# Norms in three slots, and weight tiles split by casting and accumulating transfers

## The chip, the core and the metric

The kernel runs on one core of a Trainium2 chip. The time is the device time of one execution in microseconds (us), the median of several. Its engines are TensorE (PE; its weight loads are PEld), VectorE (DVE), ScalarE (ACT), GpSimd (POOL) and SyncE (SP), each with its own queue that is worked off in order; a queue's instruction waits on semaphores of the other engines and of DMA transfers.

## The reference

One step of a decoder of two layers, for 512 new prompt tokens and 8 x 4 sample tokens (544 in all), model width 1024, in float32. Layer 0 mixes tokens by gated linear attention (GLA), layer 1 by a complex diagonal state-space layer (S5); behind each stands a squared-ReLU MLP of width 4096. Every sublayer stands between two RMS norms:

```
def _rmsnorm(x, g):
    y = xf * lax.rsqrt(jnp.mean(xf * xf, axis=-1, keepdims=True) + EPS)
    return (y * g.astype(jnp.float32)).astype(x.dtype)
...
        h = _rmsnorm(x, prm['g_pre_mix'][i])
        m = mixer(h)                       # GLA or S5
        x = x + _rmsnorm(m, prm['g_post_mix'][i])
        h = _rmsnorm(x, prm['g_pre_mlp'][i])
        f = jnp.square(jax.nn.relu(h @ prm['w_up'][i])) @ prm['w_down'][i]
        x = x + _rmsnorm(f, prm['g_post_mlp'][i])
```

## The kernel before

Features lie on the partitions, tokens along the rows: `X` is 128 x 8 x 544, eight k-slices of 128 features. The tokens are cut in half 0 (288 columns) and half 1 (256).

**Weights and jobs.** The weights are 184 tiles of 128 x 8 x 128 (512 KB). A float32 product is made of three passes in the type float32r: weight high x input high, weight high x input low, weight low x input high (`advance`, L204 to L207, 8 k-slices x 3 = 24 matmuls). A **job** is one tile for one half; `PLAN` lists the blocks of tiles and their order, 368 jobs, counted here from 0. Blocks of 8 tiles (B) run all eight tiles for half 0 and then for half 1; blocks of 4 (Q) do the same with four; the S5 input block runs five tiles for half 0, the same five for half 1, then the last three by turns.

**Splitting a tile** into `wh` (high) and `wl` (low). SP loads the raw tile into one of three buffers (`load_raw`, L97). ACT writes `wh`, the tile rounded to float32r, in two halves of 128x512 (`split_w`, L119); POOL, and in some stages DVE, subtract: `wl = raw - wh` (L126, L124). While a norm is under way (`dve_win`), POOL does all of the subtraction. `plan` (L131) decides by a table ahead of which job each half tile is split: as soon as its slot in a ring of 5 (or among 4 extra ones) is free, at most 9 jobs ahead. When the second half is split, the raw tile three further on is loaded.

**The queue order** is written by hand: `job` puts the planned splits first, then the 24 matmuls, and `finish` then the evacuation of the job's PSUM bank, the functions deferred to that job (`self.after`), and what is late. So on each engine the norm's instructions stand between the evacuations of successive jobs, and nothing overtakes.

**The norm between two sublayers** (`post`, L322). When the last tile of a block's half is done, `m_done` has summed the squares of the block's output `acc` into `S1`; a matmul by ones sums them over partitions (L258), `rsqrt` (L261) makes the factor `rp` (ACT two passes, DVE three). Then come steps of one to two k-slices each, one step a job, five steps for half 0 and at most six for half 1. A step (L336) does on DVE `xm = acc * g * rp` (L340) and `X += xm` (L343), then the step before's `xl` (`pre_lo`, L311), and on ACT `xh = X * g` (L301) and the square of `X` (L279) into the PSUM bank that `xm` had; the sum of that square into `S2` (DVE, L280) is put off to the next job. `xh` and `xl` are the inputs of the next block; the factor of the second norm (`rs`) is applied at that block's evacuations.

Such norms stand at three places where the next block needs `xh` and `xl` at once: **norm 1** between the GLA's output block (tiles 24 to 31, jobs 48 to 63) and the first MLP (tiles from 32, jobs from 64), **norm 2** between that MLP and the S5 input (tiles 96 to 103, jobs 192 to 207), and **norm 3** between the gated output of S5 (tiles 112 to 119, jobs 224 to 239) and the second MLP (tiles from 120, jobs from 240). In each, half 0's norm runs beside the jobs of half 1 of the block before, and half 1's norm beside the jobs of half 0 of the next.

Of the kernel before, what the change touches and what calls it, by code (L numbers as in the profile page):

```python
# [9 lines left out]
F32 = mybir.dt.float32  # L10
# [8 lines left out]
KD = D // 128  # L19
# [7 lines left out]
C_ID, C_ONE, C_TRI, C_END = 0, 128, 256, 384  # L27
V_PRE, V_POST, V_MPRE, V_MPOST, V_HEAD, V_GATE, V_EPS, V_END = 0, 16, 32, 48, 64, 72, 76, 77
RING, RAW, LEAD = 5, 3, 9

# [4 lines left out]
Q, B = (4, QUAD), (8, BIG)  # L37
MLP = [B, Q, Q] + [Q, Q, Q, Q] * 2 + [Q, Q, B]
PLAN = [Q] * 6 + [B] + MLP + [(8, S5IN)] + [Q, Q, B] + MLP
EXTRA_FROM = (6, 6 + len(MLP), 8 + len(MLP))  # L40


def f32(ap):
    return ap.bitcast(F32)
# [33 lines left out]
class Builder:  # L78
# [16 lines left out]


    def load_raw(self, t):  # L97
        if t < self.n_tiles:
            r = self.p_raw.tile([128, KD, 128], F32, tag="raw", name="raw")
            self.nc.sync.dma_start(r, self.io["w"][t].rearrange("p (k m) -> p k m", k=KD))  # L100
            self.raw[t] = r

    def split_w(self, t, part=None, cast_only=False):

        if part is None:
            self.split_w(t, 0)
            self.split_w(t, 1)
            return
        nc = self.nc
        r = self.raw[t]  # L110
        if part == 0 and (t, 0) not in self.is_cast:
            pool = self.p_x if self.in_x[t] else self.p_w
            self.wh[t] = pool.tile([128, KD, 128], F32R, tag="wh", name="wh")
            self.wl[t] = pool.tile([128, KD, 128], F32R, tag="wl", name="wl")
        h, l = self.wh[t], self.wl[t]
        d = self.dve_ks if self.dve_win is None else self.dve_win
        a, b, c = part * 4, part * 4 + d, part * 4 + 4
        if (t, part) not in self.is_cast:
            nc.scalar.activation(h[:, a:c], r[:, a:c], AF.Copy)  # L119
        if cast_only:  # L120
            self.is_cast.add((t, part))
            return
        if b > a:
            nc.vector.tensor_sub(l[:, a:b], r[:, a:b], f32(h[:, a:b]))  # L124
        if c > b:
            nc.gpsimd.tensor_sub(l[:, b:c], r[:, b:c], f32(h[:, b:c]))  # L126
        if part:
            del self.raw[t]
            self.load_raw(t + RAW)

    def plan(self):  # L131

        first, last, self.in_x = {}, {}, {}
        j = t = 0
        opened = 0
        ready = {}
        for b, (n, order) in enumerate(PLAN):
            if b in EXTRA_FROM:
                opened = j
            for i, _ in order:  # L140
                first.setdefault(t + i, j)
                last[t + i] = j
                j += 1
            for i in range(n):
                self.in_x[t + i] = order is BIG and i >= 4
                ready[t + i] = opened if self.in_x[t + i] else 0
            t += n
        assert t == self.n_tiles
        slots = {False: [0] * RING, True: [0] * 4}
        self.split_at = defaultdict(list)  # L150
        at = 0
        for t in range(self.n_tiles):
            free = slots[self.in_x[t]]
            soon = free.pop(0) + 1
            if t > 3:
                soon = max(soon, ready[t], first[t] - LEAD)
                at = max(soon, min(at + 2, first[t] - 5))
                assert at < first[t], t
                self.split_at[at].append((t, 0))
                self.split_at[min(at + 1, first[t] - 1)].append((t, 1))  # L160
            free.append(last[t])
        self.wjob = 0
        self.block = 0
        self.flat = [(b, h) for b, (_, order) in enumerate(PLAN) for _, h in order]
# [157 lines left out]
    def post(self, hf, g_post, g_pre, sink=None):  # L322

        nc = self.nc
        c0, c1 = HALF[hf]
        n = c1 - c0
        R = {}

        def start():
            r = self.p_t.tile([128, 288], F32, tag="rp", name="rp", bufs=1)  # L330
            self.rsqrt(self.col_sums(self.S1[hf][:, :n], n), n, 1.0 / D, r[:, :n])
            R["r"] = r

        fresh = []

        def step(ks):  # L336
            ms = [self.bank("xm")[:, :n] for k in ks]
            for k, m in zip(ks, ms):
                gk = self.vec[:, g_post + k:g_post + k + 1]
                nc.vector.scalar_tensor_tensor(m, self.acc[:, k, c0:c1], gk, R["r"][:, :n], op0=OP.mult, op1=OP.mult)  # L340
            for k, m in zip(ks, ms):
                x = self.X[:, k, c0:c1]
                nc.vector.tensor_add(x, x, m)  # L343
            if g_pre is not None:
                for k in fresh:
                    self.pre_lo(hf, k, g_pre)
                fresh[:] = ks
                for k, m in zip(ks, ms):
                    self.pre_hi(hf, k, g_pre, False, True, None, m)
            if sink:  # L350
                for k in ks:
                    sink(hf, k)

        at = self.wjob - 1
        blk = self.flat[at][0]
        nxt = [j for j in range(at, len(self.flat)) if self.flat[j][0] > blk and self.flat[j][1] == hf]
        gap = nxt[0] - at if nxt else 4
        lead = 1
        if hf:
            self.defer(lead, start)  # L360
        else:
            self.mid[self.jobs + 1].append(start)
        self.defer(0, lambda: setattr(self, "dve_win", DK[hf]))
        if hf:
            self.defer(8, lambda: setattr(self, "dve_win", None))
        slots = min(gap - 1 - lead, SL[hf])
        for i in range(slots):
            part = list(range(KD))[i * KD // slots:(i + 1) * KD // slots]
            self.defer(lead + i, lambda part=part: step(part))
        self.defer(lead + slots, lambda: step([]))  # L370
        if g_pre is not None:
            late = HL[hf]
            self.hold.update(range(self.jobs + gap, self.jobs + gap + late))
            self.before_evac[self.jobs + gap + late].append(lambda: self.pre_scale(hf))
# [42 lines left out]
    def m_done(self, m, hf, g_post, g_next, sink=None):  # L417

        c0, c1 = HALF[hf]
        n = c1 - c0  # L420
        if sink and hf:
            self.last_done(m, g_post, sink)
            return
        self.square_into(self.S1[hf][:, :n], self.acc[:, m, c0:c1], n, m == 0,
                         self.nc.vector, hf and m < KD - LT)
        if m == KD - 1:

            self.nc.scalar.activation(self.spare, self.vec[:, V_EPS:V_EPS + 1], AF.Abs_reciprocal_sqrt)
            self.post(hf, g_post, g_next, sink)
# [1132 lines left out]
```

## Time and profile before

| | us |
|---|---|
| median of 3 runs (lowest, highest) | 1340.35 (1338.58, 1344.46) |
| profiled execution | 1346.7 |
| its span, first to last instruction | 1344.9 |
| PE busy | 1293.1 |
| DVE busy | 763.9 |
| ACT busy | 621.2 |
| POOL busy | 467.4 |

The profiled execution's own time is 1.8 us over its span, and 6.35 us over the median. Its mean granted clock of TensorE is 0.984. In the rows quoted below a name like `xl<-X,vec,xh` is output and inputs; "x2" is a count; what stands in brackets is how long the engine stood idle before and who released it.

### The profile page before, as it was taken

To read this page: it belongs to the slowest core of one execution; us is meant where nothing else is said; L and a number is where in the kernel's file an instruction comes from. 1 tells how busy PE (TensorE), PEld (TensorE's weight loads), DVE (VectorE), ACT (ScalarE), POOL (GpSimd) and SP (SyncE) were. 2 spreads that over 40 slices of the span, in tenths; PEclk is the share of its full clock that TensorE was granted. 3 is DMA by queue.
4 is the path that set the end of the run, shared out by engine and by line. 5 is a ranking of instruction groups with operands and counts; after the bars stand their busy time and mean duration, and the time that the engine had idled before them with its cause. 6 is when DMAs were issued, how large, how long until landed. Compare 5 with 4: busy or idle time off the path is not lost. (4 is left out here: it accounts for less than half of the span.)

```text
span 1344.9 us, 25669 instructions
## 1 busy us (share of the span) xinstructions
PE 1293.1 (96%) x9966; PEld 1265.0 (94%) x9966; DVE 763.9 (57%) x1749; ACT 621.2 (46%) x1412; POOL 467.4 (35%) x603
## 2 busy tenths in 40 slices
PE   7999999999999999999998988998999999999996
PEld 6899999999999999999998987997999999999996
DVE  6866564678436667666567787346821332332446
ACT  6634354565426646555444343445533432432432
POOL 4443254543371111121422443443324333343241
PEclk9999899999999999999999999999999999999998
DMA  6242222322325555545315686331222223232222
GB/s 192 95 130 86 97 93 83 115 81 73 110 77 163 157 162 173 167 144 160 104 59 193 196 263 205 98 110 63 64 79 90 86 79 108 79 91 83 79 63 67
DMA packets 80681, 155.29 MB, mean 115 GB/s; under 512 B 9040, under 2 KB 45264, under 8 KB 79536
## 3 DMA queue, kind: packets, MB, share of 16 engines
q1 hardware_dynamic: 80560, 153.66, 36.9%
q8 instruction: 78, 1.28, 0.4%
q14 instruction: 43, 0.35, 0.1%
HBM read 128.17 MB, written 25.46 MB: 114 GB/s over the span
## 5 line engine op out<-in xcount | busy, mean ns | idle before, releaser
L126 POOL TENSOR_TENSOR wl<-raw,wh 128x384 fp32r<-128x384 f32 (+3 forms) x351 | 346.9, 1000 | 637.7 <-ACT wh L119 631.1
L206 PE MATMUL held<-xl,wh 128*128 128x256 f32 (+1 forms) x1344 | 393.2, 293 | 11.1 <-DVE xl L311 11.1
L206 PE MATMUL held<-xh,wh 128*128 128x256 f32 (+1 forms) x1344 | 395.2, 294 | 0.1
L206 PE MATMUL held<-xh,wl 128*128 128x256 f32 (+1 forms) x1344 | 389.9, 290 | 0.0
L206 PE MATMUL held<-hh,wh 128*128 128x256 f32 (+1 forms) x1024 | 296.2, 289 | 1.1 <-ACT acc L396 1.1
L206 PE MATMUL held<-hl,wh 128*128 128x256 f32 (+1 forms) x1024 | 296.1, 289 | 0.0
L206 PE MATMUL held<-hh,wl 128*128 128x256 f32 (+1 forms) x1024 | 294.7, 288 | 0.0
L119 ACT ACTIVATE wh<-raw 128x512 fp32r<-128x512 f32 x368 | 219.9, 621 | 125.0 <-PE held L206 75.7
L206 PEld LDWEIGHTS held<-xl,wh 128*128 128x128 f32 x1344 | 256.6, 191 | 13.9 <-DVE xl L311 13.4
L206 PEld LDWEIGHTS held<-xh,wh 128*128 128x128 f32 x1344 | 256.8, 191 | 2.8 <-issue 1.2
L206 PEld LDWEIGHTS held<-xh,wl 128*128 128x128 f32 x1344 | 256.1, 191 | 0.0
L124 DVE TENSOR_TENSOR wl<-raw,wh 128x128 fp32r<-128x128 f32 (+3 forms) x324 | 170.9, 539 | 111.5 <-ACT wh L119 104.2
L206 PEld LDWEIGHTS held<-hh,wh 128*128 128x128 f32 x1024 | 193.2, 189 | 3.0 <-ACT acc L396 1.3
L206 PEld LDWEIGHTS held<-hl,wh 128*128 128x128 f32 x1024 | 193.0, 188 | 0.1
L206 PEld LDWEIGHTS held<-hh,wl 128*128 128x128 f32 x1024 | 192.7, 188 | 0.0
L388 ACT ACTIVATE r<-r 128x256 f32<-128x256 f32 (+1 forms) x128 | 55.0, 430 | 162.2 <-DVE r L386 162.1
L398 DVE TENSOR_TENSOR acc<-held,acc 128x288 f32<-128x288 f32 (+1 forms) x96 | 42.1, 439 | 119.9 <-PE held L206 119.9
L390 DVE TENSOR_TENSOR hl<-r,hh 128x256 fp32r<-128x256 f32 (+1 forms) x128 | 60.7, 474 | 84.6 <-ACT hh L389 84.3
L386 DVE SCALAR_TENSOR_TENSOR r<-held,rs 128x256 f32<-128x256 f32 (+1 forms) x128 | 55.9, 437 | 70.7 <-PE held L206 70.2
L206 PE MATMUL held<-zl,wh 128*128 128x288 f32 (+1 forms) x240 | 69.0, 288 | 1.2 <-DVE zl L1298 1.1
L206 PE MATMUL held<-zh,wh 128*128 128x288 f32 (+1 forms) x240 | 69.5, 289 | 0.0
L206 PE MATMUL held<-zh,wl 128*128 128x288 f32 (+1 forms) x240 | 68.8, 286 | 0.0
(387 smaller groups left out, 2010.7 us busy)
## 6 DMA issues: line engine op xcount, KB each, us to landing
raw<-in_w SPq DMA_DIRECT2D x184, 512.0 KB, 3.6
S<-in_h SPq DMA_DIRECT2D x4, 1024.0 KB, 4.9
out_gla_s<-S SPq DMA_DIRECT2D x4, 1024.0 KB, 3.8
wd<-blk SPq DMA_DIRECT2D x16, 256.0 KB, 2.6
wd<-cs SPq DMA_DIRECT2D x16, 256.0 KB, 3.3
qd<-blk SPq DMA_DIRECT2D x16, 256.0 KB, 2.6
qt<-qd SPq DMA_DIRECT2D x16, 256.0 KB, 3.9
wt<-wd SPq DMA_DIRECT2D x12, 256.0 KB, 4.3
```

Of the source, the lines that this page charges most:

```text
L119: nc.scalar.activation(h[:, a:c], r[:, a:c], AF.Copy)
L124: nc.vector.tensor_sub(l[:, a:b], r[:, a:b], f32(h[:, a:b]))
L126: nc.gpsimd.tensor_sub(l[:, b:c], r[:, b:c], f32(h[:, b:c]))
L206: self.nc.tensor.matmul(ps, a[:, k], cols(b, k), start=(k == 0 and i == 0), stop=(k == KD - 1 and i == 2))
L386: nc.vector.scalar_tensor_tensor(r[:, :n], ps, 0.0, self.rs[hf][:, :n], op0=OP.max, op1=OP.mult)
L388: nc.scalar.activation(r[:, :n], r[:, :n], AF.Square)
L390: self.late.append(lambda: nc.vector.tensor_sub(hl[:, m, c0:c1], r[:, :n], f32(h)))
L398: nc.vector.tensor_add(a, ps, a)
```

## The change

It has two parts.

*Norms in three slots.* A step is cut in three: `residual` (DVE: `xm`, `X`), `high` one job later (ACT: `xh`, squares), `low` one job after that (DVE: `xl`, sums of squares). The squares go to tiles in SBUF, the first one straight into `S2`. For half 1 the number of steps is at most `gap - 3`, where it was `gap - 2`: six as before where the gap is nine jobs, three instead of four in norm 2. The squares of `acc` in half 1, but the first and the last two, are put off by a job.

*Eighteen tiles by transfers.* The tiles 32 to 39, 96, 97 and 120 to 127 have no raw load and no subtraction. POOL issues a transfer from the weights in DRAM into `wh`, which casts to float32r (`load_high`); three jobs later ACT writes `wl = -wh` in one pass of 128x1024, and POOL issues a second transfer of the same tile that adds it to `wl` (`add_low`). `plan` asks for six jobs between the first transfer and the first use.

```diff
+LANDS = 3
+BY_DMA = {*range(32, 40), 96, 97, *range(120, 128)}
...
     def load_raw(self, t):
-        if t < self.n_tiles:
+        if t < self.n_tiles and t not in BY_DMA:
...
+        if part in ("high", "low"):
+            if not cast_only:
+                (self.load_high if part == "high" else self.add_low)(t)
+            return
...
-            self.load_raw(t + RAW)
+            self.load_raw(self.raw_after(t))
+
+    def raw_after(self, t):
+        ts = [u for u in range(t + 1, self.n_tiles + RAW) if u not in BY_DMA]
+        return ts[RAW - 1]
+
+    def source(self, t):
+        return self.io["w"][t].rearrange("p (k m) -> p k m", k=KD)
+
+    def load_high(self, t):
+        pool = self.p_x if self.in_x[t] else self.p_w
+        self.wh[t], self.wl[t] = (pool.tile([128, KD, 128], F32R, tag=n, name=n) for n in ("wh", "wl"))
+        self.nc.gpsimd.dma_start(self.wh[t], self.source(t))
+
+    def add_low(self, t):
+        self.nc.scalar.activation(self.wl[t], f32(self.wh[t]), AF.Copy, scale=-1.0)
+        self.nc.gpsimd.dma_start(self.wl[t], self.source(t), accum_op=OP.add)
...
-            if t > 3:
+            if t in BY_DMA:
+                soon = max(soon, ready[t], first[t] - 3 * LANDS)
+                self.split_at[soon].append((t, "high"))
+                self.split_at[soon + LANDS].append((t, "low"))
+                assert soon + 2 * LANDS < first[t], t
+            elif t > 3:
...
-        def step(ks):
+        squares = {}
+
+        def residual(ks):
             ms = [self.bank("xm")[:, :n] for k in ks]
...
-            if g_pre is not None:
-                for k in fresh:
-                    self.pre_lo(hf, k, g_pre)
-                fresh[:] = ks
-                for k, m in zip(ks, ms):
-                    self.pre_hi(hf, k, g_pre, False, True, None, m)
...
+        def high(ks):
+            for k in ks:
+                x = self.X[:, k, c0:c1]
+                nc.scalar.activation(self.xh[:, k, c0:c1], x, AF.Copy, scale=self.vec[:, g_pre + k:g_pre + k + 1])
+            for k in ks:
+                q = self.p_t.tile([128, 288], F32, tag="sq", name="sq", bufs=5)[:, :n] if k else self.S2[hf][:, :n]
+                nc.scalar.activation(q, self.X[:, k, c0:c1], AF.Square)
+                squares[k] = q
+
+        def low(ks):
+            for k in ks:
+                self.pre_lo(hf, k, g_pre)
+            for k in ks:
+                if k:
+                    s = self.S2[hf][:, :n]
+                    nc.vector.tensor_add(s, s, squares.pop(k))
...
-        slots = min(gap - 1 - lead, SL[hf])
+        slots = min(gap - 2 - lead, SL[hf]) if g_pre is not None else min(gap - 1 - lead, SL[hf])
         for i in range(slots):
             part = list(range(KD))[i * KD // slots:(i + 1) * KD // slots]
-            self.defer(lead + i, lambda part=part: step(part))
-        self.defer(lead + slots, lambda: step([]))
+            self.defer(lead + i, lambda part=part: residual(part))
+            if g_pre is not None:
+                self.defer(lead + i + 1, lambda part=part: high(part))
+                self.defer(lead + i + 2, lambda part=part: low(part))
...
-        self.square_into(self.S1[hf][:, :n], self.acc[:, m, c0:c1], n, m == 0,
-                         self.nc.vector, hf and m < KD - LT)
+        square = lambda: self.square_into(self.S1[hf][:, :n], self.acc[:, m, c0:c1], n, m == 0,
+                                          self.nc.vector, hf and m < KD - LT)
+        if hf and 0 < m < KD - 2:
+            self.after[self.jobs + 1].insert(0, square)
+        else:
+            square()
```

ACT's queue in norm 3, half 0, before, from the evacuation of job 233 (`s`, a sigmoid; `acc` is the evacuation of job 234). Lines are those of each program; the number behind a name tells one buffer from the next.

```order
L1383 ACTIVATE s_10925<-held_10900 128x256
L279 ACTIVATE sq_10928<-acc_10158 128x256
L301 ACTIVATE xh_79<-X_78,vec_76 128x288
L279 ACTIVATE xm_10930<-X_78 128x288
L301 ACTIVATE xh_79<-X_78,vec_76 128x288
L279 ACTIVATE xm_10931<-X_78 128x288
L119 ACTIVATE wh_10896<-raw_10662 128x512
L1380 ACTIVATE acc_10158<-held_10945 128x256
```

The same place now:

```order
L1431 ACTIVATE s_10912<-held_10887 128x256
L382 ACTIVATE xh_79<-X_78,vec_76 128x288
L385 ACTIVATE S20_83<-X_78 128x288
L154 ACTIVATE wl_10811<-wh_10810 128x1024
L1428 ACTIVATE acc_10154<-held_10928 128x256
L310 ACTIVATE sq_10954<-acc_10154 128x256
```

Behind job 233 now stands the first k-slice, whose `X` DVE made behind job 232, where the second and third stood, whose `X` is made behind job 233 itself. The half tile of `wh` has become a whole pass `wl<-wh`, and the square of `acc` stands one job later.

DVE's queue at the same place before, from the product that ends the evacuation of job 233 (`acc<-acc,s`) to the step behind job 234:

```order
L1384 TENSOR_TENSOR acc_10158<-acc_10158,s_10925 128x256
L340 SCALAR_TENSOR_TENSOR xm_10930<-acc_10158,vec_76,rp_10877 128x288
L340 SCALAR_TENSOR_TENSOR xm_10931<-acc_10158,vec_76,rp_10877 128x288
L343 TENSOR_TENSOR X_78<-X_78,xm_10930 128x288
L343 TENSOR_TENSOR X_78<-X_78,xm_10931 128x288
L311 SCALAR_TENSOR_TENSOR xl_80<-X_78,vec_76,xh_79 128x288
L280 TENSOR_TENSOR S20_83<-S20_83,xm_10931 128x288
L280 TENSOR_TENSOR S20_83<-S20_83,xm_10930 128x288
L280 TENSOR_TENSOR S11_82<-S11_82,sq_10928 128x256
L340 SCALAR_TENSOR_TENSOR xm_10974<-acc_10158,vec_76,rp_10877 128x288
```

And now:

```order
L1432 TENSOR_TENSOR acc_10154<-acc_10154,s_10912 128x256
L371 SCALAR_TENSOR_TENSOR xm_10917<-acc_10154,vec_76,rp_10867 128x288
L371 SCALAR_TENSOR_TENSOR xm_10918<-acc_10154,vec_76,rp_10867 128x288
L374 TENSOR_TENSOR X_78<-X_78,xm_10917 128x288
L374 TENSOR_TENSOR X_78<-X_78,xm_10918 128x288
L342 SCALAR_TENSOR_TENSOR xl_80<-X_78,vec_76,xh_79 128x288
L371 SCALAR_TENSOR_TENSOR xm_10963<-acc_10154,vec_76,rp_10867 128x288
L374 TENSOR_TENSOR X_78<-X_78,xm_10963 128x288
L1432 TENSOR_TENSOR acc_10154<-acc_10154,s_10994 128x256
L311 TENSOR_TENSOR S11_82<-S11_82,sq_10954 128x256
L342 SCALAR_TENSOR_TENSOR xl_80<-X_78,vec_76,xh_79 128x288 x2
```

The sums into `S20` have moved behind the `xl` of their slices, and no longer stand between one step's `X` and the next one's `xm`.

POOL's queue through norm 3 and after, before (the first two rows are the end of S5's scan, the third holds the tiles up to the norm, the fourth those beside it, the fifth the rest of the program's):

```order
L1362 TENSOR_TENSOR area<-area 128x256
L1363 TENSOR_TENSOR S_82<-S_82,area 128x256
L126 TENSOR_TENSOR wl<-raw,wh 128x384 x25
L126 TENSOR_TENSOR wl<-raw,wh 128x512 x16
L126 TENSOR_TENSOR wl<-raw,wh 128x384 x111
```

And now:

```order
L133 TENSOR_TENSOR wl<-raw,wh 128x384 x24
L150 DMA wh<-in_w 128x1024 x2
L155 DMA wl<-in_w 128x1024
L150 DMA wh<-in_w 128x1024 x2
L155 DMA wl<-in_w 128x1024 x2
L150 DMA wh<-in_w 128x1024
L155 DMA wl<-in_w 128x1024
L150 DMA wh<-in_w 128x1024 x2
L155 DMA wl<-in_w 128x1024
L150 DMA wh<-in_w 128x1024
L155 DMA wl<-in_w 128x1024 x3
L133 TENSOR_TENSOR wl<-raw,wh 128x512
```

Sixteen subtractions are gone, one of the third row and fifteen of the fourth; one of 128x512 is left behind the norm, and sixteen transfers stand there instead, each tile's second one queued ahead of later tiles' first ones.

More of the change, by code (lines that the diff above doesn't have):

```diff
@@ L332, in start @@
             R["r"] = r
-        fresh = []
-        def step(ks):
+        squares = {}
+        def residual(ks):
             ms = [self.bank("xm")[:, :n] for k in ks]
```

## The prediction

> **What bounds the kernel now.** I read the page first: PE is busy for 96% of the span, so only the other 4%, and what is slow inside the 96%, can be won. The waits of PE come next; the largest of them is this row (engine and line, whom it waits for: us in total, times, longest).
>
> ```profile
> PE held L206 <- DVE xl L311: 11.1, 10, 3.2
> ```
>
> PE waits for `xl`, the low half of a normed input, so the waits are at the starts of the blocks behind the three norms that feed further blocks. Then I cut PE's stretches there, from the first matmul of a job to the first of a later one, beside two undisturbed stretches (borders, us, PE busy and matmuls, granted clock, DMA share, GB/s).
>
> ```profile
> 294.70:300.10 5.40, 4.46 (x30) 1.00 0.23 46
> 322.70:327.40 4.70, 3.44 (x29) 1.00 0.00 0
> 707.20:713.50 6.30, 4.48 (x30) 1.00 0.35 105
> 726.50:736.90 10.40, 8.25 (x52) 0.84 0.28 107
> 880.96:906.55 25.59, 25.59 (x195) 1.00 0.44 135
> 909.88:926.72 16.84, 16.84 (x146) 1.00 0.21 64
> 929.65:945.50 15.85, 10.81 (x53) 0.78 0.26 78
> 964.69:975.00 10.31, 8.22 (x52) 0.83 0.00 0
> ```
>
> Rows 5 and 6 hold 8 jobs of half 0 and 6 of half 1: 3.20 us and 2.81 us a job at a clock of 1.00. The other rows are jobs 64, 72, 192, 197+198, 240+241 and 248+249. A job behind a norm also carries column sums, which this change leaves. What one costs at full clock shows inside job 232 (start, us, operation):
>
> ```profile
> 909.04 0.65 PE L258 MATMUL sums<-S,cst 128*128 128x288 f32 x2
> 909.31 0.49 PE L206 MATMUL held<-zh,wh 128*128 128x256 f32 x1
> 909.64 0.28 PE L206 MATMUL held<-zl,wh 128*128 128x256 f32 x1
> ```
>
> From 909.04 to 909.64 where one matmul takes 0.12: about 0.5 us. Jobs 64, 192 and 240 carry two sums, jobs 72, 197 and 248 one. So the stretches lose, against their own pace:
>
> - norm 1 (before the first MLP): 5.40 - 4.2 = 1.2, and 4.70 - 3.3 = 1.4; together 2.6 us
> - norm 2 (before S5): 6.30 - 4.2 = 2.1, and 10.40 - 6.1 = 4.3; together 6.4 us
> - norm 3 (before the last MLP): 15.85 - 7.4 = 8.45, and 10.31 - 6.1 = 4.2; together 12.65 us
>
> 21.6 us in all, which is the ceiling of what the change can win. Part of it is a granted clock of 0.78 to 0.84 in the rows in which PE stood still; a wait that goes takes that with it.
>
> **Why the norms are late.** In norm 3 (905 to 975 us) two things stand in the waits.
>
> ```profile
> ACT xh L301 <- DVE X L343: 14.9, 10, 2.4
> PE held L206 <- DVE xl L311: 6.6, 5, 3.2
> ```
>
> First, ACT stands 14.9 us for the `X` that DVE has to make in the same step: a step goes DVE, ACT, and back to DVE. Second, DVE is stretched wherever POOL splits a weight tile (two POOL rows, then four of DVE):
>
> ```profile
> 934.06 1.26 POOL L126 TENSOR_TENSOR wl<-raw,wh 128x512 fp32r<-128x512 f32 x1 [3.37 <-ACT wh L119]
> 936.65 2.82 POOL L126 TENSOR_TENSOR wl<-raw,wh 128x512 fp32r<-128x512 f32 x2 [1.33 <-ACT wh L119]
> ...
> 916.49 0.43 DVE L1384 TENSOR_TENSOR acc<-acc,s 128x256 f32<-128x256 f32 x1 [3.15 <-ACT s L1383]
> 922.42 0.94 DVE L311 SCALAR_TENSOR_TENSOR xl<-X,vec,xh 128x288 fp32r<-128x288 f32 x2
> 934.28 1.32 DVE L1384 TENSOR_TENSOR acc<-acc,s 128x256 f32<-128x256 f32 x1 [1.26 <-ACT s L1383]
> 936.38 1.96 DVE L311 SCALAR_TENSOR_TENSOR xl<-X,vec,xh 128x288 fp32r<-128x288 f32 x2
> ```
>
> The same DVE operation takes 0.43 us alone and 1.32 beside POOL's subtraction, the pair of `xl` 0.94 and 1.96. DVE ends the `xl` of job 240 at 938.34, where PE, which began that job at 929.65, wanted the last ones (k = 6, 7 of 8, three quarters of 3.2 us in) at about 932.
>
> **The change, norm 3, half 0.** The eight tiles 120 to 127 no longer pass through POOL, so the stretched rows lose 0.9 to 1.0 us each. The steps become three slots: DVE's residual, one job later ACT's `xh` and squares, one job later DVE's `xl` and sums, so neither engine waits inside a slot. What is left is DVE's own work, and it has to fit. `rp`, from which it starts, ends at 912.3; one row of each kind in this window:
>
> ```profile
> 911.84 0.45 DVE L270 SCALAR_TENSOR_TENSOR rp<-na,ny 128x288 f32<-128x288 f32 x1
> ...
> L343 DVE TENSOR_TENSOR X<-X,xm 128x288 f32<-128x288 f32 x8 | 3.3, 446 | 0.1
> L280 DVE TENSOR_TENSOR S<-S,xm 128x288 f32<-128x288 f32 x7 | 3.2, 450 | 1.8 <-ACT xm L279 1.7
> ```
>
> Up to the last `xl` stand 8 `xm` and 8 `X` at about 0.45, 8 `xl` at 0.47, five sums of the new squares at 0.45, and three products and three sums of half 1 at 0.43: 7.2 + 3.8 + 2.3 + 2.6 = 15.9 us, so 928.2 at the earliest. The slots follow PE's jobs: the last `xl` stands behind job 238, which ends at 926.7 (row 6 ends there), and behind ACT's last `xh`. I put it at about 928.5, before the 932 that PE needs. The wait and the low clock behind it go: 8.45 us, of which I take 7.5.
>
> **Half 1** is tight. From `rp` at 948.41 to the last `xl` at 969.80 DVE needs 21.4 us; four rows in between are stretched:
>
> ```profile
> 947.99 0.42 DVE L270 SCALAR_TENSOR_TENSOR rp<-na,ny 128x256 f32<-128x256 f32 x1
> ...
> 950.90 1.52 DVE L311 SCALAR_TENSOR_TENSOR xl<-X,vec,xh 128x256 fp32r<-128x256 f32 x1
> 952.34 1.55 DVE L390 TENSOR_TENSOR hl<-r,hh 128x288 fp32r<-128x288 f32 x1
> ...
> 954.51 2.26 DVE L340 SCALAR_TENSOR_TENSOR xm<-acc,vec,rp 128x256 f32<-128x256 f32 x2
> ...
> 959.45 1.39 DVE L340 SCALAR_TENSOR_TENSOR xm<-acc,vec,rp 128x256 f32<-128x256 f32 x1
> ...
> 968.93 0.87 DVE L311 SCALAR_TENSOR_TENSOR xl<-X,vec,xh 128x256 fp32r<-128x256 f32 x2
> ```
>
> Against about 0.45 a piece that is 1.05 + 1.1 + 1.35 + 0.95 = 4.4 us, which leaves 17.0. `rp` ends 7.1 us after job 241 begins:
>
> ```profile
> 941.34 0.80 PE L206 MATMUL held<-xh,wh 128*128 128x288 f32 x1
> ```
>
> Seven jobs of 3.20 later job 248 begins, and wants its last `xl` 2.1 us into it: 24.5 us, against 7.1 + 17.0 = 24.1. It fits by 0.4 us, so of the 4.2 us I take 3.5. Norm 3: 11.0 us.
>
> **Norm 1** has the same shape with tiles 32 to 39: of 2.6 us I take 2.2.
>
> **Norm 2** has only tiles 96 and 97 by transfer; 98 to 100 are split on POOL as before, a few jobs sooner. Half 1 has three slots instead of four, since the block is followed after six jobs. Its rows on DVE:
>
> ```profile
> 708.13 2.50 DVE L311 SCALAR_TENSOR_TENSOR xl<-X,vec,xh 128x288 fp32r<-128x288 f32 x2
> ...
> 716.56 0.42 DVE L270 SCALAR_TENSOR_TENSOR rp<-na,ny 128x256 f32<-128x256 f32 x1
> ...
> 722.91 0.86 DVE L280 TENSOR_TENSOR S<-S,xm 128x256 f32<-128x256 f32 x2
> ...
> 730.83 0.88 DVE L311 SCALAR_TENSOR_TENSOR xl<-X,vec,xh 128x256 fp32r<-128x256 f32 x2
> ```
>
> The stretched pair of 2.50 (1.56 over the 0.94 above) falls at a time when POOL now has nothing, which brings `rp` forward by about 1.6. From `rp` to the last `xl` (716.98 to 731.71) DVE is full without any help from POOL; all that goes is three sums that now stand behind the last `xl`, 3 x 0.43 = 1.3 us. PE still waits there and still gets the low clock. 1.6 + 1.3 = 2.9 us.
>
> **The sum:** 11.0 + 2.2 + 2.9 = 16.1 us. The profiled execution took 1346.7 us (span 1344.9) and the median shown is 1340.35; I take the same 16 us off both: 1330.6 for a profiled one, **1324.3** for the median.
>
> **What is added.** On ACT one pass of 128x1024 stands where two of 128x512 stood; the row of the latter in norm 3 is
>
> ```profile
> L119 ACT ACTIVATE wh<-raw 128x512 fp32r<-128x512 f32 x17 | 10.2, 615 | 0.0
> ...
> L279 ACT ACTIVATE xm<-X 128x288 f32<-128x288 f32 x7 | 2.8, 395 | 0.0
> ...
> L275 ACT ACTIVATE S<-X 128x288 f32<-128x288 f32 x1 | 0.4, 428 | 0.0
> ```
>
> so it costs the same 1.1 to 1.2 us, now in a piece and with a wait: it needs the first transfer landed, and behind it in ACT's order stand evacuations. The squares keep their passes and go to SBUF instead of PSUM (0.43 against 0.40 us, rows 3 and 2), which is nothing. SP's queue loses 18 loads, and nothing behind them comes later. POOL issues 36 transfers, in order; the second of each tile waits for ACT there, and the next tile's first stands behind it. Neither operation is in the trace. The nearest rows are the raw loads of the same 512 KB and the queue as a whole:
>
> ```profile
> raw<-in_w SPq DMA_DIRECT2D x184, 512.0 KB, 3.6
> ...
> DMA to landing us min/median/max: 3.2/3.6/8.3
> q1 hardware_dynamic: 80560, 153.66, 36.9%
> ```
>
> Landing: no quicker than 3.2 us, and for the accumulating one, which fetches what it adds and what it adds to, at most twice the slowest load, 16.6. I take 3.6 and about 7. The plan leaves three jobs (9 us) between the first transfer and ACT's pass, and four or more from there to the first use (12 us, less some 3.5 in which ACT gets to it): both fit. Throughput: 0.369 x 16 x 1344.9 us for 153.66 MB is 1.7 us of all 16 engines for 512 KB, so a tile's two transfers are 1.7 + 3.4 = 5.1 us if the second counts double; eight tiles take 41 us of the 16 jobs (48 us) from job 231 to job 247. At zero they cost nothing; above 6 us a tile they are late.
>
> The Trainium skill, "Collectives: The Full Stack", section "The bandwidth ceiling", says that the add in a transfer costs nothing itself, but needs two reads on the same ring. No run here shows it; by it the pair is those 5.1 us, with no add on top.
>
> **Rivals.**
>
> *POOL holds DVE up all the same.* If building a transfer on POOL stretches DVE as its subtraction does, norm 3's and norm 1's collisions stay (16 transfers for 16 subtractions, 0.9 us each, a good half of them on the late path). Left are the slots' share and norm 2: about 6 us, 1334. For it: every POOL row of these windows has a stretched DVE row beside it. Against it: the issue touches none of the tiles that DVE reads. The Trainium skill, "SBUF — State Buffer", section "Who interferes with whom", says that a DVE instruction with two SBUF inputs collides with a GpSimd instruction that reads SBUF, not with one that only writes. The rows above agree with the first half; the second no trace here shows, and by it this rival falls.
>
> *ACT becomes late.* ACT's pass waits for a landing of over 9 us, or simply stands as 1.1 us ahead of an evacuation, and the slots behind it slip by a job. That gives back half 1 of norm 3 and more, and leaves 1337 to 1341, no change. It speaks for it that half 1 fits by 0.4 us only.
>
> *The accumulating transfers are slow: slower than before.* They share one queue. At 8 us a tile, eight take 64 us of the 48: 16 us of PE waiting for `wl` in norm 1 and again in norm 3, 32 lost against 16 won, 1356. It decides from 6 us a tile. Against it: the DMA share in these stretches is 0 to 0.44.
>
> **How the numbers follow.** Forecast 0.66; POOL still in the way 0.14; ACT late 0.10; slow transfers 0.10. The forecast's own range is 1319 (19 us won) to 1331. A measurement of this kernel tells 0.5% (6.7 us) from no change: faster is the forecast and half of the first rival, 0.73; the same 0.17; slower 0.10. The range that leaves out two in ten reaches from 1318 to 1339.
>
> **What will show it.** Right: PE's waits for `xl` at the starts of norms 1 and 3 are gone, the clock is 1.00 there, no DVE row of norm 3 exceeds 0.6 us, job 197 still waits. Wrong: rows "PE held <- DMA wl", or ACT waiting for `wh` from DMA (transfers); DVE rows over 1 us beside POOL's DMA rows (first rival); PE waiting for `xl` with undisturbed DVE rows (ACT late).

## The result, and the profile after

| | before | after |
|---|---|---|
| median of 6 runs each (lowest to highest), us | 1342.51 (1338.58 to 1346.79) | 1329.23 (1325.58 to 1331.35) |
| profiled execution, us | 1346.7 | 1328.09 |
| its span, us | 1344.9 | 1326.3 |

The ratio is 0.9904, with a 95% interval from 0.9887 to 0.9921: the change saves about 13 us. The prediction was 1324.3 us, with a range of 1318 to 1339.

The list of waits of the changed kernel (engine and line, whom it waits for: us in total, times, longest) has the last four of these rows; the first two are of the kernel before, where PE also waited 11.1 us for `xl`:

```profile
PE sums L258 <- DVE S L280: 2.2, 3, 1.5
ACT xh L301 <- DVE X L343: 44.8, 27, 3.6
...
PE held L237 <- DVE xl L342: 0.4, 1, 0.4
PE sums L289 <- DVE S L394: 4.5, 4, 1.3
PE sums L289 <- DVE S L311: 1.4, 1, 1.4
ACT xh L382 <- DVE X L374: 11.1, 8, 3.4
```

So PE's wait for `xl` is gone but for 0.4 us, and a smaller one has grown from 2.2 to 5.9 us: for `S`, the sums of squares, which DVE now adds behind the last `xl`, and without which PE cannot do the column sum of the new norm.

The stretches of the prediction in the changed kernel (jobs 64, 72, 192, 197+198, 240+241, 248+249; borders, us, PE busy and matmuls, granted clock, DMA share, GB/s):

```profile
288.75:292.67 3.92, 3.92 (x31) 1.00 1.10 257
315.25:319.81 4.56, 3.39 (x28) 1.00 0.00 0
699.32:706.53 7.21, 4.57 (x30) 1.00 0.37 120
719.51:727.57 8.06, 6.75 (x52) 1.00 0.15 57
921.93:929.25 7.32, 7.32 (x55) 1.00 1.08 306
948.63:956.28 7.65, 6.47 (x52) 1.00 0.21 59
```

The clock is 1.00 in all six. Jobs 64 and 240+241 are without a gap; they were 5.39 and 15.85. Row 3 is longer than before (6.27), and rows 2, 3, 4 and 6 still hold gaps of 1.2 to 2.6 us.

**Where the 13 us are.** I take the difference of the two traces' job starts, piece by piece. From job 64 to 75 it grows by 1.6 us (norm 1), from 191 to 199 by 1.4 (norm 2), from 239 to 251 by 11.2 (norm 3). That makes 14.2 us. Between 199 and 212, in the S5 stage, 1.8 us come back; in the ten traces of the experiments the same piece takes from 106.4 to 110.0 us (before 108.1), in no order that follows what was changed, so I leave it out of the account. The two spans differ by more, 18.6 us: another 5.9 us lie ahead of job 48, in GLA code that the change doesn't touch (last section).

**What is left in the gaps.** Norm 2 of the changed kernel, DVE and POOL (start, us, engine, line, operation; idle time before and who ended it):

```profile
690.82 2.58 DVE L371 SCALAR_TENSOR_TENSOR xm<-acc,vec,rp 128x288 f32<-128x288 f32 x2
...
698.62 2.06 DVE L394 TENSOR_TENSOR S<-S,sq 128x288 f32<-128x288 f32 x2
...
702.13 1.89 DVE L394 TENSOR_TENSOR S<-S,sq 128x288 f32<-128x288 f32 x2
```

```profile
691.47 1.60 POOL L133 TENSOR_TENSOR wl<-raw,wh 128x512 fp32r<-128x512 f32 x1
...
699.08 1.29 POOL L133 TENSOR_TENSOR wl<-raw,wh 128x512 fp32r<-128x512 f32 x1 [1.47 <-ACT wh L126]
702.38 1.32 POOL L133 TENSOR_TENSOR wl<-raw,wh 128x512 fp32r<-128x512 f32 x1 [2.01 <-ACT wh L126]
```

Three DVE pairs, 0.94 to 1.01 us each where nothing collides, are stretched to 1.9 to 2.6 beside the subtractions of tiles 98 to 100. Two of them are sums of squares: these now read two tiles in SBUF. In norm 3 one place is left, at 949.21, where the pair of `xl` and the two sums behind it are stretched beside POOL's subtraction of tile 128, just when job 248 needs them. Norm 1 has the same beside tile 40, at 315.82 (norm 3 first, then norm 1):

```profile
949.21 1.97 DVE L342 SCALAR_TENSOR_TENSOR xl<-X,vec,xh 128x256 fp32r<-128x256 f32 x2
951.10 1.75 DVE L394 TENSOR_TENSOR S<-S,sq 128x256 f32<-128x256 f32 x2
949.21 1.29 POOL L133 TENSOR_TENSOR wl<-raw,wh 128x512 fp32r<-128x512 f32 x1 [9.65 <-ACT wh L126]
...
315.82 1.91 DVE L342 SCALAR_TENSOR_TENSOR xl<-X,vec,xh 128x256 fp32r<-128x256 f32 x2
316.02 2.57 POOL L133 TENSOR_TENSOR wl<-raw,wh 128x512 fp32r<-128x512 f32 x2 [9.65 <-ACT wh L126]
```

### The profile page after: what moved, and what is told of

Same layout as the page of the kernel before. It is cut to its first block, busy times and chain, and to the rows that moved or that the text cites. A ratio compares the mean times of both kernels' runs of the same rounds, so it can differ in the third digit from the quotient of the medians.

```text
span 1326.3 us, 25660 instructions
## 1 busy us (share of the span) xinstructions
PE 1281.2 (97%) x9966; PEld 1256.4 (95%) x9966; DVE 748.7 (56%) x1746; ACT 618.9 (47%) x1394; POOL 445.7 (34%) x603
## 5 line engine op out<-in xcount | busy, mean ns | idle before, releaser
L133 POOL TENSOR_TENSOR wl<-raw,wh 128x384 fp32r<-128x384 f32 (+3 forms) x315 | 300.1, 964 | 552.0 <-ACT wh L126 547.1
L237 PE MATMUL held<-xl,wh 128*128 128x256 f32 (+1 forms) x1344 | 389.2, 290 | 0.4 <-DVE xl L342 0.4
L126 ACT ACTIVATE wh<-raw 128x512 fp32r<-128x512 f32 x332 | 198.4, 622 | 124.4 <-PE held L237 78.7
L237 PEld LDWEIGHTS held<-xh,wh 128*128 128x128 f32 x1344 | 254.0, 189 | 2.4 <-issue 1.4
L237 PEld LDWEIGHTS held<-xl,wh 128*128 128x128 f32 x1344 | 253.6, 189 | 1.0 <-DVE xl L342 0.6
L237 PEld LDWEIGHTS held<-xh,wl 128*128 128x128 f32 x1344 | 253.1, 188 | 0.2 <-DMA wl<-in_w 0.2
L434 DVE TENSOR_TENSOR hl<-r,hh 128x256 fp32r<-128x256 f32 (+1 forms) x128 | 56.4, 440 | 83.8 <-ACT hh L433 83.3
```

The lines of the kernel that those rows point to most:

```text
L237: self.nc.tensor.matmul(ps, a[:, k], cols(b, k), start=(k == 0 and i == 0), stop=(k == KD - 1 and i == 2))
L434: self.late.append(lambda: nc.vector.tensor_sub(hl[:, m, c0:c1], r[:, :n], f32(h)))
```

## The experiments

All times are medians of 4 to 12 runs; the ratio is to runs of the kernel before that were taken beside them. A table of job lengths from the traces (start to start, us) comes first, since most of the reading is done in it. "Both" is the changed kernel. Each kernel has one trace, of one of its executions.

| jobs | before | both | slots alone | transfers alone | transfers, high first | 23 tiles, high first |
|---|---|---|---|---|---|---|
| 64, 65 | 8.78 | 7.31 | 11.48 | 7.31 | 7.31 | 7.31 |
| 68, 69 | 6.40 | 6.40 | 6.40 | 13.41 | 7.53 | 6.40 |
| 72, 73 | 7.71 | 7.61 | 6.66 | 6.13 | 6.13 | 6.13 |
| 192, 193 | 9.65 | 10.60 | 10.76 | 11.58 | 9.64 | 7.31 |
| 197, 198 | 10.42 | 8.06 | 7.81 | 6.83 | 9.91 | 8.92 |
| 240, 241 | 15.85 | 7.32 | 9.96 | 9.46 | 9.45 | 7.32 |
| 243 to 245 | 9.60 | 9.79 | 9.60 | 16.80 | 12.57 | 9.60 |
| 248, 249 | 10.34 | 7.65 | 11.77 | 6.13 | 6.13 | 6.13 |
| median, us | 1342.51 | 1329.23 | 1342.17 | 1342.56 | 1331.65 | 1323.76 |

### Each part by itself

```diff
-BY_DMA = {*range(32, 40), 96, 97, *range(120, 128)}
+BY_DMA = set()
```

> The changed kernel with no tile by transfer (BY_DMA empty): all 184 tiles are loaded by SP and split by ACT and POOL again; the three slots and the squares in SBUF stay. Theory 1, POOL's subtractions are the larger cause: the stretched DVE rows (1.3 to 2.0 us beside POOL) are back in norms 1 and 3, job 240 takes 8 us or more again, PE waits for xl 6 to 10 us in all, and the time is 1335 to 1339 (3 to 7 us won against the kernel before, my prediction put 6). Theory 2, the waits of ACT and DVE for each other in a step are the cause: job 240 stays near 4 us, the time stays at 1329 to 1331. Theory 3, the squares in SBUF make more DVE work collide with POOL (the sums of squares now have two inputs in SBUF), which takes back what the slots win: 1340 or more.

Measured: 1342.17 us, ratio 1.0002 (0.9981 to 1.0023). Nothing is won in the medians; theory 1's 3 to 7 us and theory 2 fall, and the time is the one that theory 3 gave. In the table the slots win at jobs 240 and 197, and give back at jobs 64 and 65, at 192 and at 248. By the one trace they don't give back all of it: over the three pieces used above it is 4.5 us shorter than the trace of the kernel before (1.7 lost in norm 1, 1.5 and 4.6 won in norms 2 and 3). The medians of 12 and 23 runs don't show these 4.5 us, and their interval ends at about 2.5 us won; where the rest goes stays open. DVE's rows of norm 1 (jobs 55 to 74) by form, first of the kernel before, then of the slots alone (count, busy us, mean ns):

```profile
L311 DVE SCALAR_TENSOR_TENSOR xl<-X,vec,xh 128x288 fp32r<-128x288 f32 x8 | 5.4, 707 | 0.0
...
L280 DVE TENSOR_TENSOR S<-S,xm 128x288 f32<-128x288 f32 x7 | 3.2, 454 | 3.1 <-ACT xm L279 3.0
```

```profile
L342 DVE SCALAR_TENSOR_TENSOR xl<-X,vec,xh 128x288 fp32r<-128x288 f32 x8 | 7.8, 1008 | 0.0
L394 DVE TENSOR_TENSOR S<-S,sq 128x288 f32<-128x288 f32 x7 | 6.2, 888 | 0.3
```

The slots put `xl` and the sums where POOL subtracts: 2.4 and 3.0 us more for these two forms, against 2.2 us less for the `xm` of both halves. Of the 42 sums of squares of `X` in the whole trace, two start while POOL subtracts in the kernel before, with the square in PSUM, and none takes over 0.6 us; in the run of the slots nine do, with the square in SBUF, and all nine take 1.3 to 1.6 us. So the slots changed both how many sums meet a subtraction and where the square stands. That fits the rule of the Trainium skill, "SBUF — State Buffer", section "Who interferes with whom": a DVE instruction with at most one SBUF input doesn't contend with GpSimd (two-port modes aside), one with two contends with a GpSimd instruction that reads SBUF. The rows 454 and 888 agree with it on both sides.

The other part (the diff shows its core; the old number of steps and the sums of `acc`'s squares at their old place belong to it):

```diff
-        def residual(ks):
...
+        def step(ks):
...
+            for k, m in zip(ks, ms):
+                self.pre_hi(hf, k, g_pre, False, True, None, m)
```

> The kernel before with the eighteen tiles by transfer and nothing else: steps of DVE, ACT, DVE, squares in PSUM, sums of acc's squares at their old place. Theory 1 (POOL's subtractions are the larger cause): the DVE rows of norm 3 are undisturbed, its last xl of half 0 comes about 7 us earlier (eight POOL rows of 0.9 us each), which is nearly the 6.3 us by which it was late, so job 240 takes 4 to 6 us and the time is 1329 to 1333. Theory 2 (ACT and DVE waiting for each other in a step): ACT still waits some 30 us or more for X, job 240 takes 8 us or more, the time is 1336 to 1340. If the parts add, this run's gain and that of the slots alone make 13 us together; if either is enough, each wins nearly 13; if both are needed, they win less than 13 together.

Measured: 1342.56 us, ratio 1.0000 (0.9981 to 1.0018). Nothing again, so the parts win 13 us together and none apart. But the table says why. The collisions do go: norm 3 (jobs 231 to 249) has 15 transfers issued on POOL and no DVE row stretched beside one,

```profile
L371 DVE SCALAR_TENSOR_TENSOR xm<-acc,vec,rp 128x288 f32<-128x288 f32 x8 | 3.9, 520 | 0.0
L342 DVE SCALAR_TENSOR_TENSOR xl<-X,vec,xh 128x288 fp32r<-128x288 f32 x8 | 3.8, 510 | 0.0
```

and 1.5 us are won at job 64, 6.4 at 240 and 241, 4.2 at 248 and 249. Then 14.2 us are lost at jobs 68, 69 and 243 to 245, to a wait that the kernel before doesn't have (PE's row first, then ACT and POOL in norm 1):

```profile
PE held L237 <- DMA wl<-in_w: 9.4, 4, 3.7
```

```profile
293.55 0.88 POOL L155 DMA_DIRECT2D wl<-in_w  x1 [3.27 <-ACT acc L647]
294.10 0.90 POOL L150 DMA_DIRECT2D wh<-in_w  x1
295.22 0.87 POOL L155 DMA_DIRECT2D wl<-in_w  x1 [0.22 <-ACT acc L647]
295.80 1.39 POOL L150 DMA_DIRECT2D wh<-in_w  x2
302.76 0.90 POOL L155 DMA_DIRECT2D wl<-in_w  x1 [5.58 <-ACT wl L154]
```

```profile
301.40 1.06 ACT L154 ACTIVATE wl<-wh 128x1024 fp32r<-128x1024 f32 x1 [4.95 <-DMA wh<-in_w]
```

POOL stands for ACT's pass before each accumulating transfer, and the casting transfers of later tiles stand behind it. They then leave in a heap (five between 293.55 and 297), land late, and ACT, whose order is fixed, stands 4.95 us for one of them. ACT's passes also stand behind its waits for `X`, which are 11.1 us in the changed kernel and here

```profile
ACT xh L332 <- DVE X L374: 30.2, 24, 3.0
```

### The order on POOL

If that is the cause, it is enough to give POOL the casting transfer first, in the jobs that issue both kinds:

```diff
-        for u in self.split_at.pop(self.wjob, []):
+        for u in sorted(self.split_at.pop(self.wjob, []), key=lambda u: (u[1] == "low") - (u[1] == "high")):
             self.split_w(*u)
```

> The transfers alone, with one thing changed: where a job issues a casting and an accumulating transfer, POOL gets the casting one first. In the run of the transfers alone PE stood 7 us in norm 1 (jobs 68, 69) and 7 us in norm 3 (jobs 244, 245) for wl, and these 14 us are what it gave back. My theory: on POOL's in-order queue the accumulating transfer waits for ACT's pass wl = -wh (up to 7.0 us), the casting transfer of a later tile stands behind it, lands late, and ACT's next pass and the next accumulating transfer are late in turn. Then job 69 falls from 9.3 to 3.2 to 5 us and job 245 from 8.6 to 3.2 to 5, and the time is 1328 to 1334. Rival: ACT's own order (the pass behind xh, which waits for X of the same step) makes the accumulating transfers late whatever stands on POOL: jobs 69 and 245 keep 7 us or more, 1339 to 1343. Rival: the queue of transfers itself is full (each 512 KB takes 2.2 us of all 16 engines): then the late landings only move to other tiles and the sum of PE's waits for wl stays at 8 us or more, 1338 to 1342.

Measured: 1331.65 us, ratio 0.9915 (0.9895 to 0.9935): the transfers alone win 11 us with this line, and nothing without it. PE's wait is down to

```profile
PE held L237 <- DMA wl<-in_w: 2.9, 4, 1.4
```

and jobs 69 and 245 to 3.39 and 3.99 us. ACT no longer waits for a landing. Both rivals fall: neither ACT's own order nor the traffic was the cause of the large part. It also leaves only 2.4 us between this run and the changed kernel, and the intervals of the two ratios overlap: with eighteen tiles, what the slots add to well-ordered transfers is not clear of the noise.

### Which wait ends last behind a norm

Two runs on what the changed kernel leaves. First the order inside the last slot:

```diff
         def low(ks):
-            for k in ks:
-                self.pre_lo(hf, k, g_pre)
             for k in ks:
                 if k:
                     s = self.S2[hf][:, :n]
                     nc.vector.tensor_add(s, s, squares.pop(k))
+            for k in ks:
+                self.pre_lo(hf, k, g_pre)
```

> The changed kernel with the two parts of the last slot in the other order: DVE adds the squares first and writes xl behind that. If PE's new wait for the sums (4.5 us in four waits) were a cost of their place behind xl that can be had back, the time falls by 2 to 4 us, to 1325 to 1327. My theory: DVE is the limit there and ends at the same time, only another wait ends last; the rows 'PE sums <- DVE S' shrink to under 1.5 us, 'PE held <- DVE xl' rises by 2 to 5 us, since xl comes 0.45 us later for each sum ahead of it, and the time rises by 0 to 3 us, 1329 to 1332.

Measured: 1330.05 us, ratio 0.9911 (0.9888 to 0.9934), the same as the changed kernel. The wait for `S` of line 394 is gone, and the one for `xl`, 0.4 us in the changed kernel, is now

```profile
PE held L237 <- DVE xl L342: 5.2, 7, 1.5
```

The wait for `S` is no cost of its own: DVE ends at the same time, and another of its results comes last.

Then the tiles whose subtraction still meets the norms:

```diff
-BY_DMA = {*range(32, 40), 96, 97, *range(120, 128)}
+BY_DMA = {*range(32, 41), *range(96, 101), *range(120, 129)}
```

> The changed kernel with 40, 98, 99, 100 and 128 by transfer too, 23 tiles in all. My theory of what is left: the POOL subtractions of tiles 98 to 100 (jobs 186 to 191) stretch DVE before job 192, tile 128's before job 248, tile 40's before job 72. Then job 192 falls from 7.2 to about 5 us (PE's wait for the sums of squares, 1.3 and 1.4 us there, goes), job 248 from 4.6 to 3.3, job 72 from 4.6 to 3.5: 3 to 5 us less, 1324 to 1327. Rival, the order in the slots sets these waits (the sums stand behind the last xl, whatever POOL does): the stretched rows go, jobs 192, 248 and 72 keep all but 0.5 us of their length, 1328 to 1330. Rival, transfers crowd each other or ACT (five more passes of 1.1 us with a wait, in the fuller stage of S5): PE waits for wl, 1331 or more.

Measured: 1323.86 us, ratio 0.9862 (0.9835 to 0.9889), 5.4 us under the changed kernel and a little under the expected range. With the casting transfers first as well:

> The 23 tiles by transfer (the earlier run that took 1323.9) with the casting transfer ahead of the accumulating one where a job issues both. In that run PE hardly waited for wl, so by either theory nothing is to be had at jobs 64 to 73 and 240 to 249: 1322 to 1325. If the earlier landings let ACT make its passes at their planned jobs, its evacuations and with them job 197 (5.9 us, 1 us over the run with eighteen tiles) come earlier by up to 1 us. Rival: the casting transfer put ahead waits on POOL for a slot that PE has not yet left, and holds up the accumulating one behind it: PE waits for wl, 1326 or more.

Measured: 1323.76 us, ratio 0.9864 (0.9843 to 0.9885), no different, as expected. It is the best version found. Its stretches, as above:

```profile
289.02:292.94 3.92, 3.92 (x31) 1.00 1.09 258
315.52:318.61 3.09, 3.09 (x28) 1.00 0.00 0
698.08:702.00 3.92, 3.92 (x31) 1.00 0.99 177
714.98:723.90 8.92, 6.74 (x52) 1.00 0.33 120
917.83:925.14 7.31, 7.31 (x54) 1.00 1.09 287
944.34:950.47 6.13, 6.13 (x52) 1.00 0.00 0
```

Rows 2, 3 and 6 fall from 4.56, 7.21 and 7.65 to 3.09, 3.92 and 6.13, all without a gap. Row 4 is norm 2's half 1, where DVE has no idle time from `rp` to the last `xl`, with no subtraction and no transfer on POOL beside it; that one is DVE's own work.

### What the slots are still worth

```diff
-BY_DMA = {*range(32, 40), 96, 97, *range(120, 128)}
+BY_DMA = {*range(32, 41), *range(96, 101), *range(120, 129)}
...
-        def residual(ks):
...
+        def step(ks):
```

The diff shows a part; the line of order on POOL, as above, is in this kernel too.

> The 23 tiles by transfer with the casting transfer first, but the norms in the old steps with squares in PSUM and the sums at their old place. It asks what the three slots are worth once POOL's subtractions and its queue are out of the way. Theory 1, the slots still matter: with the old steps ACT waits some 30 us for X, its passes wl = -wh stand behind that, job 240 takes 6.1 us (3.9 with slots) and jobs 243 to 245 together 3 us too long, as in the run with eighteen tiles and the casting transfer first; 4 to 8 us over the same with slots (1323.8): 1328 to 1332. Theory 2, the slots were needed only to get ACT's passes out in time, which the order on POOL does as well: 1323 to 1326.

Measured: 1329.67 us, ratio 0.9925 (0.9906 to 0.9944), so theory 1 holds: with the old steps 0.6% is lost against 0.9864, clear of both intervals. In its trace ACT waits 32.3 us for `X` (24 times), jobs 240 and 241 take 9.46 us for 7.32, jobs 243 to 245 together 12.16 for 9.60, and 197 and 198 11.12 for 8.92.

### The squares in SBUF

```diff
-                    self.pre_hi(hf, k, g_pre, False, True, None, m)
+                    q = self.p_t.tile([128, 288], F32, tag="sq", name="sq", bufs=5)[:, :n]
+                    self.pre_hi(hf, k, g_pre, False, True, None, q)
```

> The kernel before with the squares of X in SBUF instead of PSUM, nothing else (steps and subtractions as before). Theory: a sum of squares with both inputs in SBUF is stretched beside POOL's subtraction, one with an input in PSUM is not (0.450 and 0.416 us on average in the kernel before, 0.606 and 0.567 in the run of the slots alone). That is 2.1 us more DVE work in norm 3, and as much in norms 1 and 2 in proportion to their collisions; where PE waits for DVE it comes through: 1 to 5 us slower than before, 1343 to 1347, and the sums' mean duration rises to 0.55 us or more. It is then what the slots alone gave back. Rival: where the square stands does not matter (the sums stay at 0.42 to 0.45 us, or the stretch falls beside other work): within 1 us of before.

Measured: 1346.92 us, ratio 1.0032 (1.0016 to 1.0048): slower by about 4 us, in the expected range. But the sums' mean over the whole run is 0.455 and 0.449 us, not the 0.55 expected; in norms 1 and 3 one sum each is stretched, since in the old order few sums meet a subtraction. So moving the squares costs something under POOL's subtractions, and less of it than I thought lies in the sums themselves. How the loss of the slots alone divides between the squares and the moved `xl` stays open: three slots with squares in PSUM were not tried. Nor were the squares of `acc` that the change puts off by a job tried apart from the slots.

### The price of a transfer

Two runs with a third transfer for each of the eighteen tiles. In the first, the casting transfer is issued twice into the same tile:

```diff
         self.nc.gpsimd.dma_start(self.wh[t], self.source(t))
+        self.nc.gpsimd.dma_start(self.wh[t], self.source(t))
```

> The changed kernel with each of the eighteen casting transfers issued twice in a row into the same tile: three transfers a tile for two, the same result. It asks from which price the transfers decide. My prediction's rule was that they are late above 6 us a tile. The trace of the changed kernel gives 6.3% of 16 engines' span for 36 transfers, 2.3 us of all 16 engines each, 4.6 us a tile; three make 7.0. By that rule PE waits for wl in norms 1 and 3, about 8 us each (8 tiles x 1.0 us over 6): 1340 to 1348. Rival: there is slack beyond the 6 us, since the transfers of the second half are needed later than 3.2 us apart, or two transfers of one queue overlap: PE's waits for wl stay under 2 us, 1328 to 1331.

Measured: 1390.78 us, ratio 1.0354 (1.0329 to 1.0379), far over both expectations, and not a measurement of traffic: the second transfer into a tile waits on POOL until the first has landed.

```profile
POOL wh L151 <- DMA wh<-in_w: 86.6, 15, 9.4
...
ACT wl L155 <- DMA wh<-in_w: 57.1, 12, 9.7
```

It shows instead what waits on POOL's queue cost here: these 86.6 us and the 57.1 us that ACT stood for the same landings came through together as 62 us over the changed kernel. The second run sends the third transfer to DRAM, where nothing waits for it:

```diff
         self.nc.gpsimd.dma_start(self.wh[t], self.source(t))
+        self.nc.gpsimd.dma_start(self.junk[t], self.io["w"][t])
```

> The changed kernel with a third transfer for each of the eighteen tiles: POOL issues, behind the casting transfer into wh, one more of the same 512 KB with the same cast into DRAM that nothing reads and nothing waits for. It takes the place of the run with the casting transfer twice, in which POOL stood 86.6 us for the first landing, so that it measured a wait and not the traffic. By my rule (late above 6 us of all engines a tile; two transfers take 4.6, three 7.0) PE waits for wl in norms 1 and 3, 5 to 10 us each: 1339 to 1350. Rival, the landings have slack since ACT's pass stands three jobs behind and the first use four more: landings rise from 6.4 and 5.7 us to 8 to 11, PE's waits for wl stay under 2 us, 1328 to 1332.

Measured: 1339.40 us, ratio 0.9991 (0.9977 to 1.0006): 10 us lost against the changed kernel (12 by the ratios), at the lower end of what my rule gave. PE's waits for `wl` are 6.5 us in all, where the rule gave 5 to 10 in each norm. These waits, then the transfers of this run, and last those of the changed kernel (KB each, median us from issue to landing):

```profile
PE held L238 <- DMA wl<-in_w: 6.5, 4, 2.0
```

```profile
wh<-in_w POOLq DMA_DIRECT2D x18, 512.0 KB, 7.4
junk<-in_w POOLq DMA_DIRECT2D x18, 512.0 KB, 8.3
wl<-in_w POOLq DMA_DIRECT2D x18, 512.0 KB, 7.9
...
wh<-in_w POOLq DMA_DIRECT2D x18, 512.0 KB, 6.4
wl<-in_w POOLq DMA_DIRECT2D x18, 512.0 KB, 5.7
```

Jobs 68 and 69 take 9.93 us for 6.40, jobs 244 and 245 10.42. Landings of 7.4 and 7.9 us for 6.4 and 5.7 are enough to make `wl` late, so the changed kernel stands near the limit. This run does not tell the traffic from POOL's queue: each third transfer also takes 0.74 us of POOL and stands ahead of the next one there.

## Why the prediction was right, and where it was off

**Norm 3** (11.0 us predicted, 11.2 in the traces). Half 0: jobs 240 and 241 shrink by 8.5 where I took 7.5 of 8.45. I had sized DVE's own work a little short: an `xm` takes 0.52 us and an `xl` 0.51 (rows of the transfers alone), where I had 0.45 and 0.47. The last `xl` ends at 921.6, 17.2 us behind the end of `rp`; I had 16.2 from 912.3 to 928.5, and what counted, that it comes before PE wants it, holds with 2.7 us to spare. Half 1: 2.7 us for 3.5. What is missing is the pair of 1.97 us beside tile 128, a subtraction that I had not followed into the moved slot, and with it my sign "no DVE row of norm 3 exceeds 0.6 us" did not come true. With that tile by transfer jobs 248 and 249 lose all of 4.2 us. The two halves missed by 1.0 and 0.8 us in opposite directions; that their sum came out within 0.2 is luck.

**Norm 1** (2.2 predicted, 1.6 found). Job 64 lost its gap; job 72 kept it: its last `xl` pair, at 315.82, takes 1.91 us beside tile 40's subtraction. With tile 40 by transfer the job takes 3.09 us. The same omission as in norm 3.

**Norm 2** (2.9 predicted, 1.4 found). The step that failed is "falls at a time when POOL now has nothing". Tiles 98 to 100 are split a few jobs sooner, and there they meet an `xm` pair and two pairs of sums, which by the change read two inputs in SBUF. So job 192 became 0.95 us longer, not 1.6 shorter. The run with 23 tiles bears it out: job 192 falls to 3.92. The second half of the step, that DVE alone fills half 1 and PE still waits at job 197, held: 5.01 us in the changed kernel and 5.88 with no subtraction near.

**The base.** 4.9 us lie between the prediction and the median. 16.1 us predicted against 13.3 between the medians make 2.8 of them; the rest is that the kernel before measured 1342.51 in six runs, where I had 1340.35 from three.

**"POOL holds DVE up all the same"** fell: transfers issued on POOL stretch no DVE row here. In the changed kernel 20 `xm` and `xl` rows overlap a transfer's row on POOL and no subtraction, and the longest takes 0.52 us. But the price that I put on this rival, 6 us left for slots and norm 2, took the parts as a sum. The runs give 0 us (0.9981 to 1.0023) for the slots alone.

**"ACT becomes late" and "slow transfers"** did not happen in the changed kernel, but for one wait of ACT of 1.3 us for a landing, and both happened as soon as the slots were taken away: the transfers alone lost 14 us to `wl`. It was not the 8 us a tile that I had assumed as its price, but the wait on POOL that I had named in passing ("the next tile's first stands behind it") and not priced. My argument against slow transfers, a DMA share of 0 to 0.44 in these stretches, did not hold either: the share is 1.10 and 1.08 now in jobs 64 and 240 with 241 (above 1 because a packet's whole time counts where it starts). My limit of 6 us a tile was somewhat too high, as far as the one run with a third transfer tells. By the row of the queue in the changed kernel's page,

```profile
q0 software_dynamic: 5184, 18.88, 6.3%
```

36 transfers take 0.063 x 16 x 1326.3 us, which is 2.3 us of all 16 engines each and 4.6 a tile, near the 5.1 that I had; with a third (7.6% of 1340.5 us for 54) it is 5.7 a tile, and there PE already waits.

## What to carry to other kernels

Two parts whose medians each show nothing can win together, when each removes the wait that the other one runs into; test them apart before you credit either, and read in the trace where each gives back what it won. A transfer that waits for an engine belongs behind those that wait for nothing in its queue: one line of order was worth 11 us here without the slots, and nothing with them. When an operand moves from PSUM to SBUF, look again at which subtractions on POOL it now meets.

## What the hardware showed beside that

The GLA stage, the same code in every kernel here, takes from 224.6 to 231.8 us in the twelve traces, in no order that follows what was changed. The stretch from 12.00 to the start of job 48, first before, then after:

```profile
12.00:243.27 231.27, 228.19 (x1669) 0.96 0.31 102
```

```profile
12.00:237.35 225.35, 222.20 (x1671) 0.98 0.32 105
```

The difference is the granted clock. It falls to half for 3.4 us at a time, while PE is fully busy; of the kernel before, in that stage:

```profile
62.40:65.80 3.40, 3.40 (x17) 0.50 0.00 0
69.20:72.60 3.40, 3.40 (x16) 0.50 0.52 154
```

There are six such pieces in that stage of the kernel before and three in that of the changed one. Over all twelve traces, job 0 to job 48 takes 221.1 to 221.3 us with three pieces (seven traces), 224.3 with five (one) and 225.8 to 226.1 with six (four). What decides how many there are was not found. The difference is nearly half the effect studied, so two profiles are compared from job to job, and not by their spans.

Landings of transfers issued on POOL were slower than I had estimated for the first kind: 6.4 us for the casting one (3.6 taken), 5.7 for the accumulating one (about 7 taken), against 3.7 for the same 512 KB from SP's queue. The Trainium skill, "DMA: Bandwidth & Descriptors", section "Anatomy of one DMA — SWDGE (gpsimd) path", fits 2.0 us plus the bytes at 436 GB/s to such a transfer, an estimate of 3.2 us for 512 KB; the measured 6.4 and 5.7, of transfers that cast or add and follow each other closely, decide here.
